# Closing steps of the last attention block in another PSUM bank of a hybrid encoder layer

## The chip, the cores and the metric

The kernel runs on one core of a Trainium2 chip. The core has a matrix engine (PE, with its weight loads shown as PEld), a vector engine (DVE), a scalar engine (ACT), a general engine (POOL) and a queue engine that issues transfers (SP). Matrix products land in PSUM, which this kernel divides into eight banks of 128 x 512 float32. The metric is the device time of one execution in microseconds; the median over several runs counts.

## The reference

One encoder layer on x of 2048 x 1024 float32. A combined input projection feeds two groups of heads whose outputs are concatenated, projected and added to the input:

```python
h = x @ w_in                                   # split into the pieces below
o_a = gla_branch(g_q, g_k, g_v, g_gate, ...)   # gated linear attention, 4 heads, both directions
o_b = mla_branch(m_cq, m_ckv, m_kr, m_gate, positions, ...)
mixed = concatenate([o_a, o_b]) @ w_out        # 1024 x 1024
x = layer_norm(ALPHA * x + mixed, ln_g, ln_b)

# inside mla_branch, for each head and block of queries:
s = qn @ k_nope.T + qr @ k_r.T
p = softmax(s)
o = (p @ v) * silu(gate)
```

The part that matters here is the end of the second branch: for each head and block of queries the row sums of the exponentials, their reciprocal, and the product with the value weights; and then the output projection with its layer norm.

## The kernel before

Every float32 product is made of three matmuls of rounded halves (a high part and a low part of each operand), which the helper `mm3` issues (L368 to L370). High parts are made on ACT (`hi`, L336), low parts on DVE or POOL (`lo`, L342).

The kernel has four stages: a sweep over 16 chunks of 128 rows backward, a sweep forward in pairs of chunks, the attention, and the output projection. The attention goes over 16 blocks (4 heads times 4 groups of 512 queries), each with 8 pairs of key tiles. The order of everything in it is written out: each step has a place in a list, the list is sorted, and `in_order` chains the instructions of every engine in that order. After the list ends, only ACT, POOL and SP stay chained (`fixed`, with `LATE_ORDER`); PE and DVE are ordered by the scheduler from there.

PSUM in this stage: `pM`, `pO`, `pX` and `pA` have one bank each, `pS` has two tiles of two banks. A tile can be written only when the last reader of the tile that lay in its place is done.

- `pA` (tag "ap") holds the running row sums of a block, and in the last block also `rt`.
- `pX` (tag "x") holds, block by block, the transposed row maxima `mx`, the transposed row sums `sx` and the output product `y`.
- The output projection of a chunk takes two halves of 512 columns. Even chunks from 4 on use the single banks `pM` (tile `pmb`, first half) and `pX` (tile `px`, second half); odd chunks use one tile of `pS` (`po`). A half is 24 matmuls.

The last block, number 15, has its closing steps between the output chunks 4 to 7, because its work ends after the output projection has begun:

- after chunk 4: `tot` copies the running sums out of pA (DVE), `oh` and `ol` split the block's product `o`;
- after chunk 5: `tsum` transposes the sums into `sx` (PE), `rcp` reduces them to `rc` and takes the reciprocal (DVE, L1402 and L1403);
- after chunk 6: `turn` transposes `rc` into `rt` in pA (PE, L1414);
- after chunk 7: `y` multiplies by the value weights (PE), `yc` copies the result (ACT, L1443) and stores it (SP), `rows` copies `rt` (ACT, L1420) and stores it (SP).

Around them, for each chunk c in that order: `split(c + 2)` (ACT and POOL prepare the operands `oh` and `ol` of a later chunk, with the gate's products L1623 between), `load(c + 4)` (SP), `product(c)` (PE, with the residual sums of DVE, L1671 and L1672), and `finish(c)` (DVE: mean and variance L1680, L1681, then L1683; ACT: L381 and L382, Ln and Exp for the inverse root; DVE: L387 to L390, L1686; SP: the store L1687). Chunks 12 to 15 read what `rows` and `yc` have stored.

Of the kernel before, what the change touches and what calls it, by code (L numbers as in the profile page):

```python
# [9 lines left out]
F32 = mybir.dt.float32  # L10
# [8 lines left out]
P = 128  # L19
# [8 lines left out]
QB = 512  # L28
# [36 lines left out]
    tot=11.2,  # L65
    tsum=12.04,
    rcp=13.55,
    keep=14.21,
    oh=12.34,
    ol=12.99,  # L70
    y=16.55,
    yc=16.9,
# [255 lines left out]
class K:  # L328
# [930 lines left out]
    def attention(self):  # L1259
# [4 lines left out]
        with ExitStack() as ctx:  # L1264
# [4 lines left out]
            pM, pO, pX, pA, pS = bank("pM"), bank("pO"), bank("pX"), bank("pA"), bank("pS", 2)  # L1269
            blocks = [(h, b) for b in range(NQB) for h in range(H)]  # L1270
            nb = len(blocks)
# [111 lines left out]
            def tot(i):  # L1383
# [5 lines left out]
                V.tensor_tensor(d["ap"], d["ap"], d["as"][:, 1], ALU.add)  # L1389
                V.tensor_tensor(d["as"][:, 0], d["ap"], d["as"][:, 0], ALU.add)  # L1390

            def tsum(i):
                d = stt[i]
                d["x"] = pX.tile([P, 4, P], F32, tag="x", name=f"sx{i}")
                for e in range(4):
                    nc.tensor.transpose(d["x"][:, e], d["as"][:, 0, e * P:(e + 1) * P], self.ident)

# [35 lines left out]
            def y(i):  # L1433
                h, b = blocks[i]
                d = stt[i]
                d["y"] = pX.tile([P, QB], F32, tag="x", name=f"y{i}")
                hs = slice(h * P, (h + 1) * P)
                self.mm3(d["y"], wv_h[:, hs], wv_l[:, hs], d["oh"], d["ol"])

# [24 lines left out]
            def at(f, i, j=None):  # L1464
                p = PLACE_LAST.get(f, PLACE[f]) if i == nb - 1 else PLACE[f]
                return p[j] if isinstance(p, tuple) else p

            own = (("tot", tot), ("tsum", tsum), ("rcp", rcp), ("keep", keep), ("oh", oh), ("ol", ol), ("y", y), ("yc", yc))
            for i in range(nb):
                for j in range(NP):  # L1470
# [51 lines left out]
            def load(c):  # L1522
                if c < NCH:
                    rest[c] = dict(c=c)
                    op.load(rest[c])

            def split(c):
                if c < NCH:
                    op.hi(rest[c], 0)
                    op.lo(rest[c], 0)  # L1530
                    op.gate(rest[c])
                    op.hi(rest[c], 1)
                    op.lo(rest[c], 1)
# [18 lines left out]
            for c in range(4, NCH):  # L1552
                with fixed():
                    split(c + 2)
                    load(c + 4)
                    if 4 < c < NCH - 1:
                        op.load_res(rest[c + 1])
                    op.product(rest[c])
                    op.finish(rest[c])
                with self.after(*last.values()), fixed():  # L1560
                    for f in {4: (tot, oh, ol), 5: (tsum, rcp), 6: (turn,), 7: (y, yc, rows)}.get(c, ()):
                        f(nb - 1)


# [191 lines left out]
```

## Time and profile before

| what | value |
|---|---|
| median of 3 runs | 1356.33 us (1353.56, 1356.33, 1356.91) |
| profiled execution, its own time | 1357.8 us |
| its span, first to last instruction | 1356.0 us |
| mean granted clock of PE | 0.989 |
| output projection alone, 1190 to 1356 us | PE busy 150.42 us, DVE 142.51, ACT 22.04, POOL 64.77 |
| attention, 700 to 1190 us | PE busy 488.63 of 490 us |

Times inside the trace count from the start of the span. A row of the instructions in order of time gives the start, the duration, the engine, the line, the operation, output and inputs, and a count where several are merged; square brackets give an idle time ahead of the instruction and what ended it. Matmuls overlap: one of 128 x 512 shows 0.39 us but the next starts 0.23 us after it, so starts are compared here, not durations. The granted clock is 1.00 when PE runs at full speed.

### The profile page before, as it was taken

How to read it: one execution, taken by the hardware profiler on the slowest of the kernel's cores; microseconds unless marked ns; L12 is line 12 of the kernel's file. 1: busy time of each engine (PE TensorE's matmuls, PEld its weight loads, DVE VectorE, ACT ScalarE, POOL GpSimd, SP SyncE). 2: the span in 40 equal slices, each digit the busy share in tenths (PEclk: the TensorE clock that was granted, in tenths of full speed). 3: DMA queues.
4: the chain of work that ended last, by engine and by line, in shares of the span. 5: the costliest groups of instructions: out<-in, count | busy, mean ns of one | idle time of the engine just before them, and what ended most of it. 6: DMA issues, size and time to landing. Idle time of an engine off the chain costs nothing.

```text
span 1356.0 us, 20031 instructions
## 1 busy us (share of the span) xinstructions
PE 1308.2 (96%) x7121; PEld 1143.4 (84%) x7121; DVE 950.4 (70%) x1683; ACT 814.1 (60%) x1339; POOL 805.7 (59%) x509
## 2 busy tenths in 40 slices
PE   7799999999999999999999999999999999998997
PEld 6789899999979999999878888888888887786885
DVE  6656755554585544445598888888888888379996
ACT  6646456555575655555587887778888888411110
POOL 2532332424257666663088888889999999745440
PEclk9899999999998999999999999999999999998999
DMA  7322132222284555664701111121123210466642
GB/s 239 97 57 84 51 87 74 70 71 64 78 294 147 172 195 188 200 202 132 219 0 39 40 40 39 40 55 55 55 64 96 59 39 9 117 221 199 209 156 93
DMA packets 108268, 147.39 MB, mean 109 GB/s; under 512 B 17314, under 2 KB 62758, under 8 KB 108168
## 3 DMA queue, kind: packets, MB, share of 16 engines
q1 hardware_dynamic: 99416, 143.46, 34.3%
q0 software_dynamic: 832, 2.62, 0.5%
q8 instruction: 56, 0.92, 0.3%
q10 hardware_dynamic: 7920, 0.03, 0.3%
q14 instruction: 44, 0.36, 0.1%
HBM read 94.93 MB, written 51.15 MB: 108 GB/s over the span
## 4 chain that ended last, share of the span: by engine, by line
PE 47%; DVE 3%; DMA 2%; ACT 1%; issue 1%; POOL 1%; SPq 0%; DVEq 0%; ACTq 0%; POOLq 0%
PE pS L1293 4%; PE pS L1296 4%; PE pS L1295 4%; PE pS L1297 4%; PE pS L1294 4%; PE o L368 4%; PE o L369 4%; PE o L370 4%; PE po L369 2%; PE po L370 2%; PE po L368 2%; DMA of<-ob_s 1%; PE px L368 1%; PE px L369 1%; PE px L370 1%; DVE rr L1686 1%
## 5 line engine op out<-in xcount | busy, mean ns | idle before, releaser
L342 POOL TENSOR_TENSOR pl<-s,ph 128x1024 fp32r<-128x1024 f32 x128 | 307.0, 2414 | 67.5 <-ACT ph L336 62.1
L1315 DVE TENSOR_TENSOR rm<-pS,rm 128x512 f32<-128x512 f32 x210 | 144.8, 690 | 44.7 <-ACT s L1302 39.5
L1302 ACT ACTIVATE s<-pS 128x1024 f32<-128x1024 f32 x128 | 131.4, 1026 | 68.2 <-PE pS L1297 66.8
L1339 DVE TENSOR_TENSOR s<-s,mb 128x1024 f32<-128x1024 f32 x128 | 151.2, 1212 | 9.1 <-PE mb L1333 9.0
L336 ACT ACTIVATE ph<-s 128x1024 fp32r<-128x1024 f32 x128 | 135.0, 1056 | 16.8 <-PE o L370 16.1
L1343 ACT ACTIVATE s<-s 128x1024 f32<-128x1024 f32 x128 | 131.4, 1050 | 13.4 <-DVE s L1339 13.3
L368 PE MATMUL ipa<-wah,xah 128*128 128x384 f32 (+1 forms) x384 | 132.0, 344 | 7.4 <-ACT wah L336 7.4
L838 POOL TENSOR_TENSOR Us<-Us,cw 128x512 f32<-128x512 f32 x16 | 18.2, 1137 | 202.0 <-DVE Us L835 172.7
L370 PE MATMUL ipa<-wah,xal 128*128 128x384 f32 (+1 forms) x384 | 126.7, 330 | 0.0
L369 PE MATMUL ipa<-wal,xah 128*128 128x384 f32 (+1 forms) x384 | 126.3, 329 | 0.0
L1293 PE MATMUL pS<-qh,ckvT_h 128*128 128x512 f32 x256 | 103.7, 405 | 0.7 <-ACT s L1343 0.4
L368 PE MATMUL o<-ph,vh 128*128 128x512 f32 x256 | 102.6, 401 | 0.0
L370 PE MATMUL o<-ph,vl 128*128 128x512 f32 x256 | 101.3, 396 | 0.0
L1296 PE MATMUL pS<-rh,krs 128*128 128x512 f32 x256 | 101.2, 395 | 0.0
L369 PE MATMUL o<-pl,vh 128*128 128x512 f32 x256 | 101.1, 395 | 0.0
L1295 PE MATMUL pS<-qh,ckvT_l 128*128 128x512 f32 x256 | 100.8, 394 | 0.0
L1297 PE MATMUL pS<-rl,krs 128*128 128x512 f32 x256 | 100.7, 393 | 0.0
L1294 PE MATMUL pS<-ql,ckvT_h 128*128 128x512 f32 x256 | 100.6, 393 | 0.0
L1366 DVE TENSOR_TENSOR ap<-ap,s 128x512 f32<-128x512 f32 x120 | 83.1, 692 | 6.3 <-ACT s L1343 4.4
L368 PEld LDWEIGHTS ipa<-wah,xah 128*128 128x128 f32 x384 | 74.7, 195 | 8.3 <-ACT wah L336 7.7
L342 POOL TENSOR_TENSOR ol<-of,oh 128x512 fp32r<-128x512 f32 x32 | 43.0, 1344 | 64.0 <-ACT oh L336 64.0
L369 PEld LDWEIGHTS ipa<-wal,xah 128*128 128x128 f32 x384 | 74.7, 195 | 0.9 <-DVE wal L342 0.4
(319 smaller groups left out, 3912.9 us busy)
## 6 DMA issues: line engine op xcount, KB each, us to landing
xcf<-xT_dram SPq DMA_DIRECT2D x16, 512.0 KB, 4.1
xr<-x_dram SPq DMA_DIRECT2D x16, 512.0 KB, 6.2
out_dram<-rr SPq DMA_DIRECT2D x32, 256.0 KB, 2.0
xaf<-xT_dram SPq DMA_DIRECT2D x14, 512.0 KB, 4.2
qdb<-qd_s SPq DMA_DIRECT2D x16, 256.0 KB, 3.9
SU<-su_s SPq DMA_DIRECT2D x16, 256.0 KB, 4.2
oib<-oi_s SPq DMA_DIRECT2D x16, 256.0 KB, 4.8
ub<-u_s SPq DMA_DIRECT2D x16, 256.0 KB, 3.7
```

What stands on the lines that cost most here:

```text
L336: return nc.scalar.activation(dst, src, AF.Copy).ins
L342: return e.tensor_tensor(dst, src, hi.bitcast(F32), ALU.subtract).ins
L368: mm(out, ah, bh, start=start, stop=False)
L369: mm(out, ah, bl, start=False, stop=False)
L370: mm(out, al, bh, start=False, stop=stop)
L1293: mm(ps[:, e], kh, qh, start=True, stop=False)
L1294: mm(ps[:, e], kh, ql, start=False, stop=False)
L1295: mm(ps[:, e], kl, qh, start=False, stop=False)
L1296: mm(ps[:, e], kr, rh, start=False, stop=False)
L1297: mm(ps[:, e], kr, rl, start=False, stop=True)
L1315: V.tensor_tensor(d["rm"], src[:, e], d["rm"], ALU.max)
L1339: V.tensor_tensor(s, s, d["mb"][:, None, :].to_broadcast([P, 2, QB]), ALU.subtract)
```

## The change

In the last block, `sx` and `y` are allocated in pA in place of pX; the other 15 blocks are as before. Since `rt` lies in pA too, `rows` (which reads it) is issued ahead of `y` and `yc`.

```diff
+            def close(i, shape, name):
+                p, tag = (pA, "ap") if i == nb - 1 else (pX, "x")
+                return p.tile(shape, F32, tag=tag, name=name)
+
             def tsum(i):
                 d = stt[i]
-                d["x"] = pX.tile([P, 4, P], F32, tag="x", name=f"sx{i}")
+                d["x"] = close(i, [P, 4, P], f"sx{i}")
...
             def y(i):
...
-                d["y"] = pX.tile([P, QB], F32, tag="x", name=f"y{i}")
+                d["y"] = close(i, [P, QB], f"y{i}")
...
                 with self.after(*last.values()), fixed():
-                    for f in {4: (tot, oh, ol), 5: (tsum, rcp), 6: (turn,), 7: (y, yc, rows)}.get(c, ()):
+                    for f in {4: (tot, oh, ol), 5: (tsum, rcp), 6: (turn,), 7: (rows, y, yc)}.get(c, ()):
                         f(nb - 1)
```

The built instructions are the same in number on every engine. On DVE and POOL their order is the same; on ACT and on SP the instruction of `rows` and that of `yc` change places; on PE the three matmuls of `y` stand after the first 16 matmuls of `pmb` of chunk 8 instead of ahead of them. Six lines are added above `tsum`, so lines behind it have numbers that are 6 higher afterwards (L1402 is L1408, L1414 is L1420, L1420 is L1426, L1443 is L1449).

## The prediction

> **What bounds the kernel now.** I read the page first, then the waits of the last stage, then that stage's windows, and last the instructions in order of time on PE, DVE, ACT, POOL and SP between 1226 and 1282 us. The page's engine row (busy us, share of the span), then the waits from 1180 us on (who waited for whom: us in total, times, longest):
>
> ```profile
> PE 1308.2 (96%) x7121; PEld 1143.4 (84%) x7121; DVE 950.4 (70%) x1683; ACT 814.1 (60%) x1339; POOL 805.7 (59%) x509
> ```
>
> ```profile
> DVE rr L1671 <- PE po L370: 7.8, 4, 5.6
> ...
> PE px L368 <- DVE rc L1402: 5.9, 1, 5.9
> DVE rr L1671 <- PE px L370: 4.1, 2, 3.2
> ```
>
> PE is busy for 96% of the span, and in the last stage its matmuls wait once: px, the second half of output chunk 6, waits 5.9 us for rc, the row-sum reduction of the last attention block. Later DVE waits for PE (7.8 and 4.1 us), so a microsecond that PE loses or wins here reaches the end. The windows (busy us of each engine, granted clock in the last columns) show the hole and what follows it:
>
> ```profile
> core 0: us, PE busy (x) PEld busy (x) DVE busy (x) ACT busy (x) POOL busy (x), PEclk, DMA share, GB/s
> 1230.00:1240.00 10.00, 4.13 (x19) 3.13 (x18) 9.90 (x20) 2.04 (x5) 5.40 (x4) 0.86 0.67 208
> 1240.00:1250.00 10.00, 10.00 (x37) 7.92 (x38) 9.79 (x13) 1.56 (x4) 5.19 (x4) 0.80 0.62 199
> 1250.00:1260.00 10.00, 10.00 (x46) 8.24 (x45) 9.66 (x14) 1.56 (x4) 5.23 (x4) 1.00 0.61 198
> ```
>
> PE has 4.13 us of work in the first ten; in the next ten it is full, but at a granted clock of 0.80. DVE is full in all three: 9.90, 9.79, 9.66. It runs behind PE, and rc stands in its queue behind chunk 5's residuals.
>
> ```profile
> 1226.06 0.68 DVE L1671 SCALAR_TENSOR_TENSOR rr<-xr,px 128x512 f32<-128x512 f32 x1
> ...
> 1239.09 0.67 DVE L1402 TENSOR_REDUCE rc<-sx 128x4 f32<-128x512 f32 x1
> ...
> 1239.79 0.17 DVE L1403 RECIPROCAL rc<-rc 128x4 f32<-128x4 f32 x1
> ```
>
> ```profile
> 1233.55 0.39 PE L370 MATMUL pmb<-woh,ol 128*128 128x512 f32 x1
> 1239.80 0.79 PE L368 MATMUL px<-woh,oh 128*128 128x512 f32 x1 [5.87 <-DVE rc L1402]
> 1240.39 0.63 PE L369 MATMUL px<-wol,oh 128*128 128x512 f32 x1
> ...
> 1243.38 0.63 PE L370 MATMUL px<-woh,ol 128*128 128x512 f32 x1
> ...
> 1247.32 0.27 PE L1414 MATMUL rt<-ident,rc 128*4 128x128 f32 x1
> 1247.34 0.48 PE L368 MATMUL po<-woh,oh 128*128 128x512 f32 x1
> ...
> 1258.35 0.40 PE L368 MATMUL y<-ofh,wv_h 128*128 128x512 f32 x1
> ...
> 1259.06 0.39 PE L368 MATMUL pmb<-woh,oh 128*128 128x512 f32 x1
> ...
> 1264.52 0.39 PE L368 MATMUL px<-woh,oh 128*128 128x512 f32 x1
> ...
> 1269.96 0.39 PE L368 MATMUL po<-woh,oh 128*128 128x512 f32 x1
> ```
>
> The first fence is DVE, the second PE (start, duration, line, what). The cause is the shared bank: sx lies in pX, so px of chunk 6 cannot start before rc has read sx, although the bank's previous px was read at 1226.06 + 0.68 = 1226.74. Two prices come from these rows. At full clock 24 matmuls take 1264.52 - 1259.06 = 5.46 us, 0.2275 us each. After the hole they come every (1243.38 - 1240.39) / 7 = 0.427 us for a while, and the 24 of px take 1247.32 - 1239.80 = 7.52 us. So the hole costs 5.87 us of standing and 7.52 - 5.46 = 2.06 us of slow clock.
>
> **The change part by part.** No instruction is added or removed; DVE's and POOL's orders are the same. Three things move.
>
> First, sx goes to pA. It overwrites the running sums, which were copied out long before, so no wait comes from that. px of chunk 6 is then held only by the residual that ended at 1226.74, and starts at 1233.55 + 0.23 = 1233.78. Its 24 matmuls end at 1239.24. Next on PE is rt, the transpose of rc, which needs the reciprocal: 1239.79 + 0.17 = 1239.96, so PE stands 0.8 us and rt runs at about 1240.0. Chunk 7 took 1258.35 - 1247.34 = 11.01 us and ends at 1251.05 instead of 1258.35. Up to here the gain is 7.3 us: 5.87 + 2.06 less the short wait. It is hidden from nobody, and its cover holds: pmb of chunk 8 needs the bank read at 1247.61 and operands finished at 1247.13 (rows below), both before 1251.05.
>
> Second, y goes to pA as well, the bank in which rt lies, and pA has one buffer. So y must wait for rows, the ACT copy of rt (L1420), where before it waited for nothing late. The change puts rows ahead of yc on ACT, but ACT's order is written out, and rows stays behind Ln and Exp (L381, L382) of chunk 7.
>
> Third, in the built order y now stands on PE behind 16 matmuls of pmb of chunk 8. Queued behind it are 8 of pmb, 24 of px, and everything after.
>
> ```profile
> 1247.61 0.67 DVE L1671 SCALAR_TENSOR_TENSOR rr<-xr,pmb 128x512 f32<-128x512 f32 x1
> ...
> 1255.89 2.53 DVE L1686 SCALAR_TENSOR_TENSOR rr<-rr,ln_r,lnb 128x512 f32<-128x512 f32 x2
> 1258.55 1.28 DVE L1671 SCALAR_TENSOR_TENSOR rr<-xr,po 128x512 f32<-128x512 f32 x2
> ...
> 1261.31 0.15 DVE L1681 TENSOR_SCALAR u<-mv 128x1 f32<-128x1 f32 x1
> ```
>
> ```profile
> 1261.50 0.20 ACT L381 ACTIVATE ln_l<-u 128x1 f32<-128x1 f32 x1 [5.00 <-DVE u L1681]
> 1261.74 0.20 ACT L382 ACTIVATE ln_y<-ln_l 128x1 f32<-128x1 f32 x1
> 1261.85 0.58 ACT L1443 ACTIVATE yc<-y 128x512 f32<-128x512 f32 x1
> 1262.33 0.25 ACT L1420 ACTIVATE rt<-rt 4x128 f32<-4x128 f32 x1
> 1262.48 0.62 ACT L336 ACTIVATE oh<-of 128x512 fp32r<-128x512 f32 x1
> ```
>
> ```profile
> 1245.85 1.28 POOL L342 TENSOR_TENSOR ol<-of,oh 128x512 fp32r<-128x512 f32 x1 [0.74 <-ACT oh L336]
> ...
> 1268.15 1.30 POOL L342 TENSOR_TENSOR ol<-of,oh 128x512 fp32r<-128x512 f32 x1 [0.74 <-ACT oh L336]
> ```
>
> These are DVE, ACT and POOL. When does rows run? Ln waits for u of chunk 7 at 1261.31 + 0.15, the end of a DVE chain that PE does not pace: DVE is full, and the only gap ahead of it is 1258.55 - (1255.89 + 2.53) = 0.13 us, where it just met the end of chunk 7. An earlier chunk 7 gives back at most about 0.2 us. So rows takes yc's slot: start between 1261.65 and 1261.85, end between 1261.9 and 1262.1. I take 1262.0, and y at 1262.05, since px came 0.04 us after rc's end (1239.09 + 0.67).
>
> PE reaches y at 1251.05 + 16 x 0.2275 = 1254.7, so it stands 7.35 us. What is left of chunk 8 is 3 + 8 + 24 = 35 matmuls, 7.96 us at full clock. A hole of 7.35 us is longer than the one that brought the slow clock, so I add the same 2.06. Chunk 8 ends at 1262.05 + 7.96 + 2.06 = 1272.07, where before chunk 9 started at 1269.96: **2.1 us later**. The gain of 7.3 is spent, and the restart lies 22.25 us later with 20.15 us less work behind it.
>
> The slow clock's premium is the unsure term. From below it is 0 (clock kept: chunk 8 ends at 1270.0, no change); from above it is all 35 matmuls at 0.427, 7.0 us. I take the one after the nearest hole, 2.06; a spell one and a half times as long would cost 3.1. The Trainium skill, "TensorE: Matmul & The Clock Gate", Part 1, says that the clock is halved after an idle window of about 3.4 us and restored after a busy one, and that these windows run freely; an estimate by that page is 3.4 to 6.8 us at half rate after the restart, a premium of 1.7 to 3.4 us, and about as much for the sum. The trace agrees with the lower part of it, with 2.06. The section on HAM oscillation of that page warns against idle gaps over 3.4 us, and against this change it says that a gap of that kind stays.
>
> Then the rest:
>
> ```profile
> 1268.42 0.38 SPq L1444 DMA_DIRECT2D ob_s<-yc  x1
> 1268.89 0.35 SPq L1421 DMA_DIRECT2D r_s<-rt  x1
> ```
>
> ```profile
> 1286.38 2.65 POOL L1623 TENSOR_TENSOR of<-of,gr 128x512 f32<-128x512 f32 x2
> ```
>
> ```profile
> 1270.16 0.69 DVE L1671 SCALAR_TENSOR_TENSOR rr<-xr,px 128x512 f32<-128x512 f32 x1 [0.88 <-PE px L370]
> ...
> 1281.04 1.28 DVE L1671 SCALAR_TENSOR_TENSOR rr<-xr,po 128x512 f32<-128x512 f32 x2 [1.35 <-PE po L370]
> ...
> 1346.32 1.28 DVE L1671 SCALAR_TENSOR_TENSOR rr<-xr,po 128x512 f32<-128x512 f32 x2 [5.61 <-PE po L370]
> ```
>
> On ACT, oh of chunk 10 (1262.48) is queued behind yc, which now follows y: 1262.05 + about 1.5 for three slow matmuls, 0.4 to drain the last, and 0.58 for yc, so it starts near 1264.4, some 1.9 us later. Its last low part then ends near 1268.15 + 1.30 + 1.9 = 1271.4; chunk 10 starts a chunk of 10.9 us after 1272, so 11 us cover it. The two stores to DRAM swap places on SP; both stand behind chunk 7's outputs as before, and who reads them gates chunk 12 at 1286.38, 17 us after. They cost nothing. Nor does px of chunk 8 win by losing its wait for yc: yc had ended at 1262.43, before 1264.52. DVE already waited for px of chunk 8 (0.88), for chunk 9 (1.35) and for chunk 15 (5.61), so the 2.1 us pass through to the end.
>
> Sum: the profiled execution took 1357.8 us (span 1356.0) and would take 1359.9. The runs' median is 1356.33, 1.5 below it, so the forecast for the median is 1356.33 + 2.1 = **1358.4 us**, up 0.15%. About 0.3%, 4.07 us, is what a measurement of this kernel tells from no change.
>
> **The rivals.**
> *The wait at y does not bind (faster).* If rows were done by 1254.7, say because ACT reached it before Ln, PE would keep its 7.3 us, and DVE's later waits (0.88 to 5.61) would absorb them: 1349.0 us. Against it is that rows has stood behind Ln and Exp in ACT's written order and that u comes at 1261.46. For a partial gain, each microsecond by which u is earlier counts one. Chance 0.06.
>
> *The slow clock is new to the median (slower).* The runs lie between 1353.56 and 1356.91, the profiled execution at 1357.8. If most runs of before kept their clock through 5.87 us, only the profiled one paid 2.06, and the changed kernel, with 7.35 us, always does: 2.1 + 2.06 = 4.2 later, 1360.5; with a spell one and a half times as long, 5.2 later, 1361.5. It decides if the hole that surely halves the clock lies between 5.9 and 7.35 us. By Part 1 of the page of the Trainium skill named above (free windows of 3.41 us) a hole of 5.87 holds a whole window in 7 cases of 10 and one of 7.35 always; no run here shows it. Against this rival:
>
> ```profile
> 48.90 0.33 PE L817 MATMUL Op<-VV,Al 128*128 128x128 f32 x1 [3.16 <-DVE Al L342]
> ```
>
> ```profile
> 48.00:56.00 8.00, 7.10 (x43) 7.10 (x44) 5.25 (x11) 5.36 (x10) 5.64 (x4) 0.79 0.39 75
> ```
>
> A hole of 3.16 us was already followed by a granted clock of 0.79, early in the kernel. Chance 0.20.
>
> *The change does not reach its aim.* Something else holds px of chunk 6 until about 1239.8, or y's wait ends so that both cancel: 1356.3. The early read of the bank speaks against it. Chance 0.04.
>
> **How the numbers follow.** The forecast has 0.70, of which 0.02 may lie past 0.3%. Faster is the first rival, 0.06; slower the second and that 0.02, 0.22; within 0.3% the rest, 0.72. The range runs from 1355.2 (premium near 0, and a microsecond of the spread of the runs) to 1361.5 (the second rival with the longer spell).
>
> **What would show it.** Right: no wait of px for rc; a wait of about 0.8 us of rt; y's first matmul waiting 7 to 7.5 us for ACT's L1426 (rt's copy); matmuls 0.43 us apart behind it; chunk 9 starting near 1272; DVE's u of chunk 7 still near 1261.4. Wrong: y not waiting, or u of chunk 7 more than a microsecond earlier (then faster), or chunk 9 starting after 1274 (then slower).

## The result and the profile after

| | before | after |
|---|---|---|
| median of the runs | 1356.30 us (1353.29 to 1358.14, 22 runs) | 1357.87 us (1355.33 to 1360.16, 22 runs) |
| ratio after to before, 95% interval | 1 | 1.0015, 1.0008 to 1.0021 |
| profiled execution, its own time | 1357.8 us | 1355.57 us |
| profiled execution, span | 1356.0 us | 1353.8 us |

The kernel became slower, by 1.57 us in the medians (0.12%) and by 0.15% in the ratio formed round by round, whose interval excludes no change. The two spans say the opposite: the profiled execution of after is 2.2 us shorter. So the spans cannot be laid over each other as they stand. The common event to count from is the first matmul of sx; nothing ahead of it is changed. It starts at 1227.88 us before and at 1224.18 after; the 3.70 us were won in stages that are alike in both, and say only how much executions differ. All comparisons below are times since sx.

The page's engine row of after (busy us, share of the span) and its waits from 1180 us on (who waited for whom: us in total, times, longest):

```profile
PE 1305.1 (96%) x7121; PEld 1140.9 (84%) x7121; DVE 948.2 (70%) x1683; ACT 814.0 (60%) x1339; POOL 804.9 (59%) x509
```

```profile
DVE rr L1677 <- PE po L370: 10.0, 5, 5.6
...
PE y L368 <- ACT rt L1426: 7.0, 1, 7.0
...
DVE rr L1677 <- PE px L370: 5.0, 2, 3.2
...
PE rt L1420 <- DVE u L1687: 0.8, 1, 0.8
```

The 5.9 us that px waited for rc are gone, and in their place stands one wait of 7.0 us: y for rows, the ACT copy of rt. The wait of rt is there too, 0.8 us; the profile names u as its releaser, but rt reads rc, whose reciprocal (DVE row below) ends at 1236.29, 0.15 us before rt starts. u runs on DVE right behind it, and the trace does not tell the two apart. DVE's waits for PE grew from 7.8 and 4.1 us to 10.0 and 5.0. The windows of after (busy us of each engine, granted clock behind them):

```profile
core 0: us, PE busy (x) PEld busy (x) DVE busy (x) ACT busy (x) POOL busy (x), PEclk, DMA share, GB/s
1230.00:1240.00 10.00, 9.23 (x43) 7.33 (x42) 9.93 (x15) 1.56 (x4) 5.98 (x5) 1.00 0.70 206
1240.00:1250.00 10.00, 10.00 (x46) 8.29 (x45) 9.72 (x15) 1.56 (x4) 4.49 (x5) 1.00 0.64 202
1250.00:1260.00 10.00, 3.00 (x10) 2.17 (x9) 9.69 (x18) 1.26 (x5) 3.38 (x3) 0.72 0.55 187
1260.00:1270.00 10.00, 10.00 (x43) 8.17 (x43) 4.36 (x9) 1.88 (x4) 5.12 (x4) 0.94 0.65 216
```

The hole of PE has moved two windows on: 4.13 us of work in the first window became 9.23, and now the third has 3.00. DVE is as full as before ahead of the hole (9.93, 9.72, 9.69) and has a hole of its own behind it, 4.36 us of work in ten. PE, ACT and DVE of after in order of time (start, duration, line, what, and in brackets the idle time before and its releaser):

```profile
1224.18 0.60 PE L1402 MATMUL sx<-ident,acc 128*128 128x128 f32 x4
...
1229.85 0.39 PE L370 MATMUL pmb<-woh,ol 128*128 128x512 f32 x1
1230.07 0.39 PE L368 MATMUL px<-woh,oh 128*128 128x512 f32 x1
...
1236.44 0.27 PE L1420 MATMUL rt<-ident,rc 128*4 128x128 f32 x1 [0.77 <-DVE u L1687]
...
1247.46 0.39 PE L368 MATMUL pmb<-woh,oh 128*128 128x512 f32 x1
...
1258.25 0.79 PE L368 MATMUL y<-ofh,wv_h 128*128 128x512 f32 x1 [7.00 <-ACT rt L1426]
1258.84 0.63 PE L369 MATMUL y<-ofl,wv_h 128*128 128x512 f32 x1
...
1261.36 0.39 PE L370 MATMUL pmb<-woh,ol 128*128 128x512 f32 x1
...
1267.71 0.39 PE L368 MATMUL po<-woh,oh 128*128 128x512 f32 x1
```

```profile
1257.60 0.20 ACT L381 ACTIVATE ln_l<-u 128x1 f32<-128x1 f32 x1 [4.75 <-DVE u L1687]
1257.84 0.20 ACT L382 ACTIVATE ln_y<-ln_l 128x1 f32<-128x1 f32 x1
1257.94 0.25 ACT L1426 ACTIVATE rt<-rt 4x128 f32<-4x128 f32 x1
1259.93 0.60 ACT L1449 ACTIVATE yc<-y 128x512 f32<-128x512 f32 x1 [1.74 <-PE y L370]
1260.42 0.62 ACT L336 ACTIVATE oh<-of 128x512 fp32r<-128x512 f32 x1
```

```profile
1236.12 0.17 DVE L1409 RECIPROCAL rc<-rc 128x4 f32<-128x4 f32 x1
...
1257.41 0.15 DVE L1687 TENSOR_SCALAR u<-mv 128x1 f32<-128x1 f32 x1
```

px of chunk 6 follows the last pmb by 0.22 us. Chunk 8's first pmb starts 23.28 us after sx; before, what followed chunk 7 (y) started at 30.47: PE was 7.19 us ahead there. Then y stands for rows. rows ends at 1257.94 + 0.25 = 1258.19, and y starts 0.06 us later, 34.07 us after sx. Its neighbours show the cause: Ln waits 4.75 us for DVE's u, and rows can only follow. From sx to chunk 9's first po it is now 43.53 us, before 42.08: 1.45 us lost. From that po to the end of the span it is 1353.8 - 1267.71 = 86.09 us, before 86.04. So the loss lies in this stretch, and it reaches the end undiminished.

### The profile page after: what moved, and what is told of

Same layout as the page of the kernel before. It is cut to its first block, busy times and chain, and to the rows that moved or that the text cites. A ratio compares the mean times of both kernels' runs of the same rounds, so it can differ in the third digit from the quotient of the medians.

```text
span 1353.8 us, 20034 instructions
## 1 busy us (share of the span) xinstructions
PE 1305.1 (96%) x7121; PEld 1140.9 (84%) x7121; DVE 948.2 (70%) x1683; ACT 814.0 (60%) x1339; POOL 804.9 (59%) x509
## 4 chain that ended last, share of the span: by engine, by line
PE 46%; DVE 4%; DMA 2%; ACT 1%; issue 1%; POOL 1%; SPq 0%; DVEq 0%; ACTq 0%; POOLq 0%
PE pS L1293 4%; PE pS L1296 4%; PE pS L1295 4%; PE pS L1297 4%; PE pS L1294 4%; PE o L368 4%; PE o L369 4%; PE o L370 4%; PE po L369 1%; PE po L370 1%; PE po L368 1%; DVE rr L1692 1%; DMA of<-ob_s 1%; DMA xr<-x_dram 1%; PE pmb L369 1%
## 5 line engine op out<-in xcount | busy, mean ns | idle before, releaser
L368 PE MATMUL pz<-xch,wzh 128*128 128x256 f32 x256 | 75.1, 293 | 0.0
```

The costliest lines, as they stand in the source:

```text
L368: mm(out, ah, bh, start=start, stop=False)
```

## The experiments

The theory: px's 7.2 us are won, and are lost again because y's new bank holds rt, and rows, which has to read rt first, stands on ACT behind Ln and Exp of chunk 7, which DVE paces; the rest of the loss is the slow clock of the restart. The rivals: the loss comes from y's late place on PE or from what queues behind it, or the slow clock is new to after. The times are medians; a ratio is formed within the rounds against the kernel before on the same chip, so it is not just the quotient of two medians. "Since sx" is from sx's first matmul to the end of the span in the profiled execution.

| run | median (runs) | ratio to before, 95% | since sx |
|---|---|---|---|
| before | 1356.30 (22) | 1 | 128.12 |
| after | 1357.87 (22) | 1.0015 (1.0008 to 1.0021) | 129.62 |
| e1_rows_early | 1348.75 (5) | 0.9936 (0.9922 to 0.9949) | 120.22 |
| e7_y_in_pO | 1347.33 (5) | 0.9946 (0.9933 to 0.9960) | 120.80 |
| e2_sx_only | 1356.93 (11) | 1.0001 (0.9990 to 1.0012) | 128.39 |
| e3_y_only | 1357.49 (11) | 1.0001 (0.9992 to 1.0010) | 128.34 |
| e6_rows_only | 1356.33 (11) | 1.0002 (0.9994 to 1.0011) | 128.45 |
| e4_fill_after | 1356.32 (11) | 1.0002 (0.9992 to 1.0012) | 128.76 |
| e5_fill_before | 1354.18 (11) | 0.9986 (0.9977 to 0.9994) | 126.36 |

**rows ahead of Ln and Exp.** The kernel after, with rows one chunk earlier in ACT's written order:

```diff
-for f in {4: (tot, oh, ol), 5: (tsum, rcp), 6: (turn,), 7: (rows, y, yc)}.get(c, ()):
+for f in {4: (tot, oh, ol), 5: (tsum, rcp), 6: (turn, rows), 7: (y, yc)}.get(c, ()):
```

> The changed kernel, but rows (the ACT copy of rt and its store) is issued right after turn, so on ACT it stands behind Ln and Exp of chunk 6 in place of chunk 7, and y stands on PE ahead of pmb of chunk 8. My theory (y waits for rows, and rows only for its place behind u of chunk 7): rows runs about 10.6 us earlier, y waits under 1 us, PE keeps the 7.3 us that the early px of chunk 6 brings, about 6.8 us faster than before (1349.5 us, ratio 0.995), and no matmul runs at half clock behind y. Rival (DVE is the bound, PE's lead is lost at the next bank): PE stands later, at pmb or px of chunk 8 or 10, for DVE's residuals, and the time stays within 2 us of before.

Measured: 0.9936, 1348.75 us, and 7.9 us less since sx than before. Waits from 1180 us on, and ACT in order of time:

```profile
PEld y L368 <- ACT rt L1426: 0.4, 1, 0.4
```

```profile
1246.16 0.20 ACT L382 ACTIVATE ln_y<-ln_l 128x1 f32<-128x1 f32 x1
1246.27 0.25 ACT L1426 ACTIVATE rt<-rt 4x128 f32<-4x128 f32 x1
...
1255.45 0.58 ACT L1449 ACTIVATE yc<-y 128x512 f32<-128x512 f32 x1
```

rows runs at 1246.27, one chunk earlier, and y's 7.0 us shrink to 0.4 us on the weight load. No matmul waits 0.4 us or more after 1180. This one place in the order turns the change from 1.5 us lost to some 8 us won, and the prediction's first rival (no wait at y, 1349.0 us) describes this version. It and the next are the fastest here.

**y in a third bank.** The kernel after, with sx in pA but y in pO, so that y has nothing to do with rt and rows:

```diff
-d["y"] = close(i, [P, QB], f"y{i}")
+p, tag = (pO, "o") if i == nb - 1 else (pX, "x")
+d["y"] = p.tile([P, QB], F32, tag=tag, name=f"y{i}")
```

> The changed kernel, with rows where the change has it, but y in the bank of pO, whose last reader (the split of o) is long done; sx stays in pA. My theory (it is the shared bank with rt that makes y wait): y waits for nothing, px of chunk 8 neither, PE has no hole after 1200 us but under 1 us at rt, about 6.8 us faster than before (1349.5 us, ratio 0.995), as with the early rows. Rival (the early rows itself, or its place on ACT ahead of oh of chunk 9, made the fast variant fast): within 2 us of before.

Measured: 0.9946, 1347.33 us. Its PE, and its longest wait of a matmul from 1180 on:

```profile
1247.17 0.40 PE L368 MATMUL y<-ofh,wv_h 128*128 128x512 f32 x1
...
1258.79 0.39 PE L368 MATMUL po<-woh,oh 128*128 128x512 f32 x1
```

```profile
PE rt L1420 <- DVE u L1688: 0.6, 1, 0.6
```

```profile
1257.70 0.25 ACT L1426 ACTIVATE rt<-rt 4x128 f32<-4x128 f32 x1
```

rows, in the last row (ACT), is nearly as late here as in after (33.60 us after sx, which starts at 1224.10, against 33.76), and yet nothing is lost: y has run 10.5 us ahead of it. So the price was the meeting of the two in one bank, not the late rows in itself. Its interval and e1's overlap; which of the two is faster isn't settled.

**Each half alone.** First the kernel after with only sx in pA, and y in pX again:

```diff
-d["y"] = close(i, [P, QB], f"y{i}")
+d["y"] = pX.tile([P, QB], F32, tag="x", name=f"y{i}")
...
-for f in {4: (tot, oh, ol), 5: (tsum, rcp), 6: (turn,), 7: (rows, y, yc)}.get(c, ()):
+for f in {4: (tot, oh, ol), 5: (tsum, rcp), 6: (turn,), 7: (y, yc, rows)}.get(c, ()):
```

> Only sx goes to pA; y stays in pX and yc stays ahead of rows, as before the change. My theory: px of chunk 6 no longer waits, y follows chunk 7 at once, but now px of chunk 8 must wait for yc, which reads y from pX and stands on ACT behind Ln and Exp of chunk 7; px of chunk 8 waits about 5 us, a little less than the 7 us of y in the changed kernel, and the slow clock follows. Chunk 9 starts within 0.7 us of before: 1355.6 to 1356.4 us. Rival (the loss lies only in y's move to pA): no wait at px of chunk 8, 1349 us.

Measured: 1.0001, no difference. PE of this run, then ACT's copy of y:

```profile
1249.55 0.40 PE L368 MATMUL y<-ofh,wv_h 128*128 128x512 f32 x1
...
1255.50 0.39 PE L370 MATMUL pmb<-woh,ol 128*128 128x512 f32 x1
1260.67 0.79 PE L368 MATMUL px<-woh,oh 128*128 128x512 f32 x1 [4.79 <-ACT yc L1449]
1261.27 0.63 PE L369 MATMUL px<-wol,oh 128*128 128x512 f32 x1
...
1265.53 0.63 PE L370 MATMUL px<-woh,ol 128*128 128x512 f32 x1
...
1268.96 0.39 PE L368 MATMUL po<-woh,oh 128*128 128x512 f32 x1
```

```profile
1260.04 0.58 ACT L1449 ACTIVATE yc<-y 128x512 f32<-128x512 f32 x1
```

The wait has only another name. y starts early (at 1249.55, 22.94 us after sx), but now px of chunk 8 needs y's bank, and so yc, which stands on ACT behind the same Ln and Exp: 4.79 us, and 8.29 us for the 24 matmuls of px.

Then only y in pA, and sx in pX again:

```diff
-d["x"] = close(i, [P, 4, P], f"sx{i}")
+d["x"] = pX.tile([P, 4, P], F32, tag="x", name=f"sx{i}")
```

> Only y goes to pA, with rows ahead of yc, as in the changed kernel; sx stays in pX. My theory: px of chunk 6 waits 5.9 us for rc as before; PE comes to y only about 1262.0 in the time of the trace of before, when rows has just ended, so y waits under 0.5 us and the kernel takes as long as before, within 0.6 us (1356.3 us). Rival (y in pA costs by itself, whatever PE's lead): 1.5 us or more slower than before.

Measured: 1.0001. Its waits from 1180 us on:

```profile
PE px L368 <- DVE rc L1408: 5.7, 1, 5.7
...
PEld y L368 <- ACT rt L1426: 0.4, 1, 0.4
```

The old hole is back, and because PE is late again, y meets a rows that has nearly run. y's move to pA, its late place on PE, the exchange of rows and yc and the later oh of chunk 10 are all in this kernel, and the ratio's interval, 0.9992 to 1.0010, leaves them no cost above 0.1%. The last piece is the kernel before with rows early and no tile in another bank:

```diff
-for f in {4: (tot, oh, ol), 5: (tsum, rcp), 6: (turn,), 7: (y, yc, rows)}.get(c, ()):
+for f in {4: (tot, oh, ol), 5: (tsum, rcp), 6: (turn, rows), 7: (y, yc)}.get(c, ()):
```

> The kernel before the change with rows issued right after turn, and sx and y left in pX: one half of what the fast variant has. My theory (rows' place only matters once y lies behind it in pA): px of chunk 6 waits 5.9 us as before, the time is that of before within 0.6 us, 1356.3 us. Rival (an early rows helps by itself, by ACT's order or the earlier store): 2 us or more faster.

Measured: 1.0002, with 5.9 us of px waiting for rc as before. The order of ACT is worth nothing by itself; it is worth 0.9936 against 1.0015 only where PE comes early.

**The slow clock.** Into the hole of after go 28 matmuls into pO that nobody reads, between the first 15 of chunk 8's pmb and y:

```diff
+def fill(i, n):
+    t = pO.tile([P, QB], F32, tag="o", name=f"fill{i}")
+    for _ in range(n):
+        mm(t, wv_h[:, :P], stt[i]["oh"], start=True, stop=True)
...
+if c == 8:
+    for k in range(5):
+        op.part(rest[c], k, (0,))
+    fill(nb - 1, 28)
+    with self.after(*last.values()), fixed():
+        y(nb - 1)
+        yc(nb - 1)
...
-for f in {4: (tot, oh, ol), 5: (tsum, rcp), 6: (turn,), 7: (rows, y, yc)}.get(c, ()):
+for f in {4: (tot, oh, ol), 5: (tsum, rcp), 6: (turn,), 7: (rows,)}.get(c, ()):
...
-for k in range(NK):
+for k in range(5 if o["c"] == 8 and n == 0 else 0, NK):
```

> The changed kernel with 28 matmuls of 128x512 that nobody reads, in the free bank of pO, on PE between the first 15 matmuls of pmb of chunk 8 and y, which fill 6.4 of the 7.35 us that PE stands. y, yc and rows keep their order on ACT. My theory (the changed kernel pays a slow clock behind the hole, beside the standing, which cannot be won this way): y waits about 1 us, no matmul at 0.43 us spacing, time 1.4 to 2.1 us below the changed kernel, 1356.3 us, ratio 1.000 to before. Rival (the slow clock plays no part, 1.5 us are something else, such as the later oh of chunk 10): 1357.9 us, ratio 1.0015, as the changed kernel.

Measured: 1.0002 against after's 1.0015. Its PE:

```profile
1252.29 6.59 PE L1449 MATMUL fill<-ofh,wv_h 128*128 128x512 f32 x28
1259.74 0.51 PE L368 MATMUL y<-ofh,wv_h 128*128 128x512 f32 x1 [0.86 <-ACT rt L1426]
1260.08 0.39 PE L369 MATMUL y<-ofl,wv_h 128*128 128x512 f32 x1
...
1268.06 0.39 PE L368 MATMUL po<-woh,oh 128*128 128x512 f32 x1
```

Behind a wait of 0.86 us the next matmul starts after 0.34 us and takes 0.39, where after has 0.59 and 0.63; the granted clock between 1250 and 1270 is 1.00, where after has 0.72 and 0.94. In the trace this version is 0.86 us shorter since sx than after, and 0.81 of it shows at chunk 9's first po: the 36 matmuls from y on take 8.32 us, 0.13 more than at full clock, so 1.37 of the slow clock's 1.50 us go, but y starts 0.33 us later (34.40 us after sx) and one matmul more, 0.23 us, is left behind it. The ratios differ by 0.0013, 1.8 us, but their intervals overlap (0.9992 to 1.0012 and 1.0008 to 1.0021): the medians fit the trace and would not show the gain by themselves.

The same in before: 24 unread matmuls into pO in front of px of chunk 6.

```diff
+if o["c"] == 6 and n == 1:
+    self.fill()
```

> The kernel before the change with 24 matmuls of 128x512 that nobody reads, in the free bank of pO, on PE between pmb and px of chunk 6, where PE stands 5.9 us for rc; they take 5.5 us. My theory (the hole of before pays a slow clock too, about 2 us, in most runs): px still starts when rc is done, with no matmul at 0.43 us spacing, 1.4 to 2.1 us faster than before (1354.5 us, ratio 0.9987). Rival (most runs of before keep their clock through 5.9 us, and only the profiled one paid): no change, 1356.3 us, ratio 1.000.

Measured: 0.9986, and 1.76 us less since sx than before. Its PE:

```profile
1232.64 5.68 PE L1443 MATMUL fill<-ofh,wv_h 128*128 128x512 f32 x24
1238.84 0.50 PE L368 MATMUL px<-woh,oh 128*128 128x512 f32 x1 [0.53 <-DVE rc L1402]
...
1244.40 0.27 PE L1414 MATMUL rt<-ident,rc 128*4 128x128 f32 x1
```

The 24 matmuls of px take 1244.40 - 1238.84 = 5.56 us in place of 7.52, and the granted clock between 1230 and 1250 is 1.00, where before has 0.86 and 0.80. Work that nobody needs makes the kernel before 0.14% faster. So the slow clock is paid in the median of before, not only in its profiled execution.

## Why the prediction was right, step by step

The forecast was 1358.4 us, 2.1 above before; the median came out at 1357.87, 1.57 above. Since sx, so that the executions can be compared:

| step | predicted | after |
|---|---|---|
| px of chunk 6 behind pmb, no wait for rc | 5.90 | 5.89 |
| rt waits | 0.8 | 0.77 |
| end of chunk 7 | 23.17 | 23.28 |
| u of chunk 7 (33.43 before) | at most 0.2 earlier | 33.23, 0.20 earlier |
| y starts, behind rows | 34.17 | 34.07 |
| wait of y | 7.35 | 7.00 |
| slow clock's premium on 35 matmuls | 2.06 | 1.50 |
| chunk 9 starts | 44.19 | 43.53 |
| oh of chunk 10 later by | 1.9 | 1.64 |

The mechanism holds at every step, and e1 and e7 show that it is the cause: the gain of 7.2 us exists and is spent on the wait for rows, and each way of taking that wait out keeps it. **The term that was mis-sized is the premium**: from 1258.25 to 1267.71 the 35 matmuls take 9.46 us, 1.50 more than the 7.96 at full clock, where 2.06 had been carried over from the shorter hole. That is 0.56 of the 0.66 us by which chunk 9 came before its forecast; the other 0.10 is y itself, since u came the 0.2 us earlier that the prediction allowed at most. The holes traced in these runs gave premiums between 1.50 and 2.83 us (last section), so it is in part luck that the one carried over was only 0.56 us off. The prediction's estimate from the Trainium skill, "TensorE: Matmul & The Clock Gate", Part 1, was a spell of 3.4 to 6.8 us at half rate. The spell in after lasts from 1258.25 to 1261.36, about 3.1 us, just below that, and in e2 from 1260.67 to about 1266.4, 5.7 us, inside it.

The rival in which the wait at y does not bind gave 1349.0; it fell for the reason stated, ACT's order, and e1 is that rival made true by changing the order. The rival by which the slow clock is new to the median fell with e5. The rival of a change that misses its aim is refuted by px at 5.89 us. The pass through to the end was right to 0.05 us, and nothing showed for the two stores or the later oh.

What the prediction did not name: behind the hole DVE waits 3.71 us for a load of xr (row below). DVE then waits 1.79 us more for px, which PE has not finished, so the load costs nothing here.

## What to carry to other kernels

Before a tile moves to another bank, look up who reads the tile that lies in that bank now, and where this reader stands in the order of its engine: if something unrelated holds the reader, the moved tile will wait for it, and the old wait has only changed its name. Price a hole of PE as its standing time plus the slow restart, and look for one line of order or another bank (0.9936 and 0.9946 here) before giving a change up. One more such line was not run: the 32 matmuls that stood behind y (8 of pmb, 24 of px) do not read it, and at 0.2275 us each they are 7.28 us of work, by estimate enough to cover y's wait of 7.00 us if y came after them. Compare two traces from an event that the change does not touch: here the slower kernel had the shorter span by 2.2 us.

## What the runs showed of the hardware that was not expected

**In these traces the slow spell does not grow with the hole.** Holes of 4.79 (e2), 5.70 (e3), 5.87 (before), 5.89 (e6) and 7.00 us (after) were followed by premiums of 2.83, 2.10, 2.06, 2.33 and 1.50 us: the longest hole had the smallest, and two holes of nearly the same length (before, e6) differ by 0.27 us. Waits of 0.5 to 1.0 us (rt's in e4 and e7, y's in e4, px's in e5) kept the clock. These are single traced executions; what sets the length within them stays open.

**DVE and POOL hold each other up.** DVE of before, then POOL of before; then DVE and POOL of after:

```profile
1263.27 1.21 DVE L390 TENSOR_TENSOR ln_r<-ln_t,ln_y 128x1 f32<-128x1 f32 x1
1264.52 3.44 DVE L1686 SCALAR_TENSOR_TENSOR rr<-rr,ln_r,lnb 128x512 f32<-128x512 f32 x2
```

```profile
1263.17 1.29 POOL L342 TENSOR_TENSOR ol<-of,oh 128x512 fp32r<-128x512 f32 x1 [5.30 <-ACT oh L336]
1264.42 2.98 POOL L1623 TENSOR_TENSOR of<-of,gr 128x512 f32<-128x512 f32 x2
```

```profile
1259.38 0.16 DVE L390 TENSOR_TENSOR ln_r<-ln_t,ln_y 128x1 f32<-128x1 f32 x1
1259.57 1.41 DVE L1692 SCALAR_TENSOR_TENSOR rr<-rr,ln_r,lnb 128x512 f32<-128x512 f32 x2
...
1264.70 0.69 DVE L1677 SCALAR_TENSOR_TENSOR rr<-xr,pmb 128x512 f32<-128x512 f32 x1 [3.71 <-DMA xr<-x_dram]
...
1267.91 0.69 DVE L1677 SCALAR_TENSOR_TENSOR rr<-xr,px 128x512 f32<-128x512 f32 x1 [1.79 <-PE px L370]
```

```profile
1261.12 1.29 POOL L342 TENSOR_TENSOR ol<-of,oh 128x512 fp32r<-128x512 f32 x1 [6.93 <-ACT oh L336]
1262.37 2.66 POOL L1629 TENSOR_TENSOR of<-of,gr 128x512 f32<-128x512 f32 x2
```

Before, a product of 128 single values takes 1.21 us and ends at 1264.48, 0.02 us after POOL's 1.29 us instruction that began ahead of it; the pair behind it takes 3.44 us beside POOL's pair of 2.98 us. After, POOL comes later (its operand oh stands on ACT behind yc), and the same work of DVE takes 0.16 and 1.41 us; POOL's pair, beside a DVE that stands, takes 2.66 us. The Trainium skill, "SBUF — State Buffer", in "SBUF: two separate sides", says that a DVE instruction with two SBUF inputs and a GpSimd one (POOL here) that reads SBUF lock a shared pair of ports in turn, for a whole instruction each. These rows agree. The 3.1 us that DVE won here are worth nothing: they went into its two waits of 3.71 and 1.79 us.
